# Eight plain products instead of seven recombined ones in the first feed-forward of each layer, with more of the modulation beside it

## The chip, the cores and the metric

The kernel runs on one core of one Trainium2 chip. TensorE (PE) multiplies, VectorE (DVE) and ScalarE (ACT) work on its results and prepare its operands, GpSimd (POOL) does elementwise work and issues some of the transfers, SyncE (SP) issues the others. The metric is the device time of one execution in microseconds (us), median of several runs.

## The reference

One step of a two-layer model on 640 tokens of width 1024: 512 latent tokens and 128 context tokens. Each layer is a feed-forward, a token mixing (a state-space model, attention, a gated MLP) and a second feed-forward. Each is preceded by a norm whose shift, scale and gate come from a conditioning vector through a large linear map, the modulation (`adaln`).

```python
def swiglu_ffn(h, w_in, w_out):
    gate, up = jnp.split(h @ w_in, 2, axis=-1)
    return (jax.nn.silu(gate) * up) @ w_out

def trunk_layer(x, mod, lp, ctx_kv, ssm_init):
    sh1, sc1, g1, sh2, sc2, g2, sh3, sc3, g3 = [mod[:, i][:, None, :] for i in range(N_MOD)]
    h = modulate(rmsnorm(x, lp['norm_ffn1']), sh1, sc1)
    x = x + 0.5 * g1 * swiglu_ffn(h, lp['ffn1_w_in'], lp['ffn1_w_out'])
    ...
    x = x + 0.5 * g3 * swiglu_ffn(h, lp['ffn2_w_in'], lp['ffn2_w_out'])
    return x, ctx_state
```

`w_in` is 1024 x 5632 and `w_out` 2816 x 1024 in each feed-forward, all in float32.

## The kernel before

**Precision.** Every float32 operand is split into a high part, rounded to the engine's fast float32 form, and a low part, the rest. A product is three matmuls (`mm3`, L574): high by high (L578), high by low (L579), low by high (L580). For a weight tile of 128 x 512 ACT makes the high part (L200) and DVE the low part (L208).

**Feed-forward.** The tokens are two halves of 320, A and B. The 2816 hidden columns are 22 units of 128. A block is three to six units: first all their input products ("in"), then the output products of the block ("out"), which are added to `x` by DVE (`accumulate`, L616). The first feed-forward of a layer (f = 0, weights `f0i` and `f0o`) has six blocks of 4, 4, 4, 3, 3 and 4 units, the second (f = 1) four blocks of 6, 6, 6 and 4.

**Seven products.** Most units compute gate and up for both token halves by Winograd's form of Strassen's scheme. The unit is a 2 x 2 problem: two halves of the inner dimension, gate and up columns, token halves A and B. Seven products of 4 `mm3` each (p1 to p7, L869 to L923) replace eight. The price is sums. Sums of the activations are made once (`sums`, L508, called by `all_x_sums`). Sums of the weights are made per unit by transfers that accumulate: POOL issues them onto the loaded tile (`add`, L187, issue at L190), then the tile is split again. Sums of the results are made by ACT copies out of PSUM (L860) and DVE additions (L877 to L921). The first two units of each feed-forward take eight plain products instead: `lead_task` and `lead_rest` in the very first block, `plain_items` in the others.

**Order of the work.** A recorder writes all instructions in one pass. It keeps a model time T, which each `mm3` of 320 columns advances by 0.41 (`clock`, L97). Background work consists of generators that are resumed when T reaches their next due time:

- the modulation (`ada`, L352) is 128 tiles, each one load on SP (L362) and two products with a sum on DVE (L372). A tile comes every `ADA_STEP[stage]` of T: 24 in the input products, 4 in the output products, 12 in the mixing;
- `ssm_build` (L1168) prepares the state-space model of the layer beside its first feed-forward. Much of it is on POOL: 16 passes over the two layers, each with a chain of small operations (L1324 to L1345) that ends in a transfer of the tile `rot`;
- while a "hot" generator is active (a norm, or `all_x_sums`), the others stand still.

Weights are loaded by SP up to nine tiles ahead (`dma`, L169) and split by `splitter` (L219) some 7 of T before they are due. Each engine works through its own list in order, so an instruction that waits holds up all that stand behind it. The 4 PSUM banks `mm` hold the results that are not yet taken away.

Of the kernel before, what the change touches and what calls it, by code (L numbers as in the profile page):

```python
# [32 lines left out]
EARLY = 4  # L33
# [13 lines left out]
           [("sc", 1), ("sh", 1), ("sh", 5), ("sc", 2), ("sh", 2), ("sc", 3)] + [("w", 1)] * 4 +  # L47
           [("sh", 7), ("sc", 4), ("sh", 4), ("sc", 5), ("sc", 6), ("sh", 6), ("sc", 7)] + [("w", 2)] * 6)
SSM_STEP = 5.0
ADA_STEP = {"in": 24.0, "out": 4.0, "mix": 12.0}  # L50
GM1, GM2 = 2.2, 2.2
LEAD, LEAD_HOT = 7.0, 5.0
DMA_LAG, ADD_LAG, HIGH_GAP, HIGH_TO_LOW, LOW_TO_ADD = 5.0, 7.5, 0.7, 0.8, 1.0
# [5 lines left out]
class Kernel:  # L59
# [369 lines left out]
    def norm(self, l, i, X):  # L429
# [5 lines left out]
        p = self.ps("sA")  # L435
# [12 lines left out]
        plain = i != 1  # L448
# [15 lines left out]
        for n in range(KD + 1):  # L464
            yield 1.3
            jobs = []
            if n < KD:
                k = ks[n]
                t = xn.pop(n) if n in xn else dest(k)
                if plain:  # L470
                    hi, lo = self.lead_x(X, k)
# [19 lines left out]
            self.ready[X] = n  # L491
            if plain and n and PLAIN[X][(n - 1) // 4]:
                self.xr[PLAIN[X][(n - 1) // 4]] = (n - 1) % 4 + 1
        if plain and X == "B":
            while not self.whole:
                yield 0.4
            yield from self.all_x_sums()
# [67 lines left out]
    def start_norm(self, nxt, X):  # L565
        self.ready[X] = 0
        self.whole = False
        if nxt[1] != 1:
            self.new_x(*(("11", "21") if X == "A" else ("22", "t1", "t2", "t3", "t4")))
        elif X == "A":  # L570
            self.H = [self.place(n, F32R).rearrange("p (k t) -> p k t", k=2) for n in H_AT]
        self.norms[X] = self.spawn(self.norm(*nxt, X), 2.2, True)
# [53 lines left out]
    def opening(self, ls, stack, ops):  # L626
# [3 lines left out]
        p = self.pool("open", 1, stack=ls)  # L630
# [62 lines left out]

        self.dlimit = 0
        pull()
        self.new_x("11", "21", "22", "t1", "t2", "t3", "t4")
        ps = {}
        for c in range(2):
            for i in range(2):
# [74 lines left out]
        self.have |= {(0, 0), (0, 1)}  # L774
        for n in ("11", "21", "22"):
            self.xr[n] = 4
        for n in ("t1", "t2", "t3", "t4"):
            self.xr[n] = 0

    def lead_x(self, X, k):  # L780

# [6 lines left out]
    def ffn_items(self, l, f, nxt, bg, lead=False):  # L788

        nc = self.nc  # L790
        items = []
# [4 lines left out]
        st = {}  # L796

        def start():
            self.enter("in")
            if not lead:  # L800
                open_hid()
                start_bg()
# [161 lines left out]
        def unit_done(us, X):  # L964
            def done(n, p):
                u = us[n // 2]
                if n % 2 == 0:
                    nc.scalar.activation(temp((u, X)), p, AF.Silu)
                else:
                    v.tensor_tensor(tmp[u, X], tmp[u, X], p, op=ALU.mult)  # L970
                    high(u, X, (u, X), 1.0)
                    low(u, X, (u, X), 1.0)
            return done
# [61 lines left out]
            return [("task", [("fi", l, f, u, f"{r}{h + 1}") for u in us for r in "12"], part(X, h), 8 * len(us) * MM3[HT])  # L1035
                    for X in "AB" for h in range(2)]

        def lead_rest(u):

            def part(n):  # L1040
                def fn(w):
                    p = self.ps()[:, :HT]
                    for k in range(KD):
                        hi, lo = self.lead_x("B", k)
                        self.mm3(p, w[k // 4], slice(k % 4 * 128, k % 4 * 128 + 128), hi, lo, k == 0, k == KD - 1)
                    unit_done([u], "B")(n, p)
                return fn
            return [("task", [("fi", l, f, u, f"{n + 1}{h}") for h in "12"], part(n), KD * MM3[HT]) for n in range(2)]

# [18 lines left out]
        for u in range(NU):  # L1068
            src = {f"{n}{h}": w_in[l, u, j][:, 512 * h:512 * h + 512] for j, n in enumerate("gp") for h in range(2)}
            op = lambda name: ("fi", l, f, u, name)  # L1070

            for n, r, y in (("11", "g0", None), ("12", "g1", None), ("22", "p1", None), ("11e", "g0e", None),
                            ("12e", "g1e", None), ("s1", "p0", "p1"), ("s2", "p0", "g0"), ("s4", "p0", "g1"),
                            ("s3", "g0", "p0")):
                self.ops[op(n)] = (512, op(r), src.get(y))
                self.raws[op(r)] = (src[r[:2]], 512)
            if u < 2:
                self.ops[op("21")] = (512, op("p0"), None)
        for b, (k0, kb) in enumerate(blocks):
            for m in range(KD):  # L1080
# [1 line left out]
        items.append(("call", start))  # L1082
        for b, (u0, kb) in enumerate(blocks):
            us = list(range(u0, u0 + kb))
            if lead and b == 0:
                items.append(lead_task(us[:2]))
                items += lead_rest(us[1])
                items.append(("call", lambda: self.norms.update(B=self.spawn(self.all_x_sums(), 0.0, True))))
                units(us[2:], us[2:])
            else:  # L1090
                items.append(("call", lambda: self.enter("in")))
                if b == 0:
                    items += plain_items(us[:2])
                    us = us[2:]
                units(us, us[:EARLY] if b == 0 else [])
            items.append(("call", lambda: (self.flush(), self.enter("out"))))
            for g in ([0, 1], [2, 3], [4, 5], [6, 7]) if b < n_b - 1 else ([0, 1], [2, 3, 4, 5, 6, 7]):
                if nxt and b == n_b - 1 and g[0] == 2 and nxt[1] == 1:
                    items.append(("call", lambda: self.preload(AF.Gelu_apprx_tanh)))
                for X in "BA" if g[0] == 0 else "AB":  # L1100
                    for m in g:
                        items.append(out_task(m, X, b, kb))
                    if nxt and b == n_b - 1 and m == 7:
                        items.append(("call", lambda X=X: (done(), self.start_norm(nxt, X))))
# [907 lines left out]
```

## Time and profile before

| | |
|---|---|
| median of 3 runs | 2658.41 us (2654.63 to 2659.7) |
| profiled execution, its own time | 2652.66 us |
| its span, from the first to the last instruction | 2650.9 us |
| PE busy | 2415.9 us, 91% |
| DVE busy | 1958.7 us, 74% |
| ACT busy | 1099.2 us, 41% |
| POOL busy | 1049.6 us, 40% |
| granted TensorE clock, mean | 0.964 of full speed |

PE is the busiest engine by far, but its busy share counts matmuls whose pipelined ends are modelled, so 91% does not say that it works at its peak. Where it is slower than elsewhere for the same matmuls has to be read stage by stage. In time the profiled execution lies a little below the fastest of the three runs.

### The profile page before, as it was taken

To read this page: it belongs to the slowest core of one execution; us is meant where nothing else is said; L and a number is where in the kernel's file an instruction comes from. 1 tells how busy PE (TensorE), PEld (TensorE's weight loads), DVE (VectorE), ACT (ScalarE), POOL (GpSimd) and SP (SyncE) were. 2 spreads that over 40 slices of the span, in tenths; PEclk is the share of its full clock that TensorE was granted. 3 is DMA by queue.
4 is the path that set the end of the run, shared out by engine and by line. 5 is a ranking of instruction groups with operands and counts; after the bars stand their busy time and mean duration, and the time that the engine had idled before them with its cause. 6 is when DMAs were issued, how large, how long until landed. Compare 5 with 4: busy or idle time off the path is not lost. (4 is left out here: it accounts for less than half of the span.)

```text
span 2650.9 us, 46542 instructions
## 1 busy us (share of the span) xinstructions
PE 2415.9 (91%) x16492; PEld 2324.6 (88%) x16492; DVE 1958.7 (74%) x4355; ACT 1099.2 (41%) x2517; POOL 1049.6 (40%) x1888
## 2 busy tenths in 40 slices
PE   6779889899999989999998889989998997999999
PEld 5669888799887879999998879888998887999999
DVE  7898688876857778677788977787766578555555
ACT  5424323345444542535354324333544445343533
POOL 5306776752533340211133376867333334121210
PEclk8899999999999999999998999999999999999999
DMA  6557767664443156876745667677353313574753
GB/s 214 133 162 186 174 163 187 160 183 149 141 150 101 57 117 176 191 191 166 193 128 122 153 165 177 174 176 188 101 175 118 113 59 82 134 148 119 155 127 97
DMA packets 193867, 391.36 MB, mean 148 GB/s; under 512 B 31858, under 2 KB 51410, under 8 KB 193636
## 3 DMA queue, kind: packets, MB, share of 16 engines
q1 hardware_dynamic: 132196, 254.94, 29.9%
q0 software_dynamic: 61440, 133.47, 26.0%
q8 instruction: 130, 2.13, 0.3%
q14 instruction: 101, 0.83, 0.1%
HBM read 365.66 MB, written 23.17 MB: 147 GB/s over the span
## 5 line engine op out<-in xcount | busy, mean ns | idle before, releaser
L578 PE MATMUL mm<-hx,w 128*128 128x320 f32 x2928 | 942.5, 322 | 116.7 <-ACT hid L860 30.7
L579 PE MATMUL mm<-hx,w 128*128 128x320 f32 x2928 | 928.1, 317 | 19.3 <-DVE hx L752 10.0
L580 PE MATMUL mm<-hx,w 128*128 128x320 f32 x2928 | 928.3, 317 | 16.6 <-DVE w L208 16.5
L208 DVE TENSOR_TENSOR w<-w 128x512 fp32r<-128x512 f32 (+1 forms) x904 | 625.4, 702 | 237.0 <-ACT w L200 233.1
L200 ACT ACTIVATE w<-w 128x512 fp32r<-128x512 f32 (+1 forms) x904 | 525.4, 608 | 540.5 <-DMA w<-f0i 196.4
L578 PEld LDWEIGHTS mm<-hx,w 128*128 128x128 f32 x2928 | 569.1, 194 | 141.0 <-ACT hid L860 34.9
L579 PEld LDWEIGHTS mm<-hx,w 128*128 128x128 f32 x2928 | 569.5, 195 | 24.3 <-DVE hx L752 11.8
L580 PEld LDWEIGHTS mm<-hx,w 128*128 128x128 f32 x2928 | 568.8, 194 | 23.5 <-DVE w L208 23.5
L578 PE MATMUL mm<-hid,w 128*128 128x320 f32 x1408 | 441.5, 314 | 29.3 <-DVE x L616 24.9
L579 PE MATMUL mm<-hid,w 128*128 128x320 f32 x1408 | 437.7, 311 | 2.3 <-DVE hid L845 2.1
L580 PE MATMUL mm<-hid,w 128*128 128x320 f32 x1408 | 436.8, 310 | 0.0
L190 POOL DMA_DIRECT2D w<-f1i x160 | 142.0, 1019 | 579.3 <-DVE w L208 368.0
L372 DVE SCALAR_TENSOR_TENSOR aj<-ar,sbc 128x1024 bf16<-128x1024 f32 x256 | 315.5, 1233 | 20.6 <-DMA ar<-w_ada 19.7
L616 DVE SCALAR_TENSOR_TENSOR x<-mm,mod,x 128x192 f32<-128x192 f32 (+1 forms) x576 | 231.4, 431 | 110.3 <-PE mm L580 109.8
L578 PEld LDWEIGHTS mm<-hid,w 128*128 128x128 f32 x1408 | 266.6, 189 | 37.8 <-DVE x L616 20.0
L579 PEld LDWEIGHTS mm<-hid,w 128*128 128x128 f32 x1408 | 266.6, 189 | 4.5 <-DVE hid L845 4.5
L580 PEld LDWEIGHTS mm<-hid,w 128*128 128x128 f32 x1408 | 266.4, 189 | 0.0
L190 POOL DMA_DIRECT2D w<-f0i x160 | 147.2, 1016 | 232.1 <-DVE w L208 121.7
L867 ACT ACTIVATE hid<-hid 128x320 f32<-128x320 f32 x148 | 69.8, 471 | 195.9 <-DVE hid L893 135.7
L841 ACT ACTIVATE hid<-hid 128x320 fp32r<-128x320 f32 x176 | 82.6, 470 | 159.3 <-DVE hid L909 69.4
L1792 PE MATMUL mm<-w,hx 128*128 128x256 f32 x480 | 143.8, 299 | 0.0
L1793 PE MATMUL mm<-w,hx 128*128 128x256 f32 x480 | 137.2, 286 | 0.9 <-DVE w L208 0.9
(340 smaller groups left out, 3239.8 us busy)
## 6 DMA issues: line engine op xcount, KB each, us to landing
ar<-w_ada SPq DMA_DIRECT2D x128, 512.0 KB, 4.7
w<-f1i SPq DMA_DIRECT2D x184, 256.0 KB, 3.8
w<-f0i SPq DMA_DIRECT2D x180, 256.0 KB, 3.8
w<-f0i POOLq DMA_DIRECT2D x160, 256.0 KB, 5.5
w<-f1i POOLq DMA_DIRECT2D x160, 256.0 KB, 5.7
w<-f1o SPq DMA_DIRECT2D x96, 192.0 KB, 2.4
w<-f0o SPq DMA_DIRECT2D x64, 256.0 KB, 3.9
w<-wqkv SPq DMA_DIRECT2D x48, 256.0 KB, 4.4
```

The costliest lines, as they stand in the source:

```text
L190: nc.gpsimd.dma_start(raw[r][:, :n], src, accum_op=ALU.add)
L200: nc.scalar.activation(pair[c][0][:, :n], raw[r][:, :n], AF.Copy)
L208: nc.vector.tensor_tensor(lo[:, :n], raw[r][:, :n], hi[:, :n].bitcast(F32), op=ALU.subtract)
L372: nc.vector.scalar_tensor_tensor(jk, r, 1.0, self.sbc[:, c, :], op0=ALU.mult, op1=ALU.mult, accum_out=m[:, c, j * KD + k:j * KD + k + 1])
L578: nc.tensor.matmul(out, hi, rhs_hi, start=start, stop=False, skip_group_check=parts)
L579: nc.tensor.matmul(out, hi, rhs_lo, start=False, stop=False, skip_group_check=parts)
L580: nc.tensor.matmul(out, lo, rhs_hi, start=False, stop=stop, skip_group_check=parts)
L616: nc.vector.scalar_tensor_tensor(self.x[:, m, r0:r1], p[:, r0 - s:r1 - s], self.mod[l][:, c, g * KD + m:g * KD + m + 1], self.x[:, m, r0:r ...
L841: nc.scalar.activation(hid[u, X][0], tmp[src], AF.Copy, scale=sign)
L867: return lambda: nc.scalar.activation(t, t, AF.Silu)
L1792: nc.tensor.matmul(p[:, :256], hh, wh, start=k == 0, stop=False)
L1793: nc.tensor.matmul(p[:, :256], hh, wl, start=False, stop=False)
```

## The change

All units of the first feed-forwards now take eight plain products. `lead_rest` is renamed `plain_unit` and takes a token half; each unit is `plain_unit(u, "A") + plain_unit(u, "B")`, which use the same four split weight tiles. For f = 0 the activation sums, their tiles t1, t2 and t4, the accumulating transfers and the sums of results are gone. t3, which holds a part of B's activations, stays. The second feed-forwards keep their seven products. The modulation gets a new stage name, "plain", for the input products of f = 0, with a tile every 8 of T instead of 24.

```diff
-ADA_STEP = {"in": 24.0, "out": 4.0, "mix": 12.0}
+ADA_STEP = {"plain": 8.0, "in": 24.0, "out": 4.0, "mix": 12.0}
...
-        if plain and X == "B":
+        if i == 2 and X == "B":
             while not self.whole:
                 yield 0.4
             yield from self.all_x_sums()
...
-        def lead_rest(u):
+        def plain_unit(u, X):
 
             def part(n):
                 def fn(w):
                     p = self.ps()[:, :HT]
                     for k in range(KD):
-                        hi, lo = self.lead_x("B", k)
+                        hi, lo = self.lead_x(X, k)
                         self.mm3(p, w[k // 4], slice(k % 4 * 128, k % 4 * 128 + 128), hi, lo, k == 0, k == KD - 1)
-                    unit_done([u], "B")(n, p)
+                    unit_done([u], X)(n, p)
...
-            if lead and b == 0:
-                items.append(lead_task(us[:2]))
-                items += lead_rest(us[1])
-                items.append(("call", lambda: self.norms.update(B=self.spawn(self.all_x_sums(), 0.0, True))))
-                units(us[2:], us[2:])
+            items.append(("call", lambda: self.enter("in" if f else "plain")))
+            if b == 0:
+                if lead:
+                    items.append(lead_task(us[:2]))
+                    items += plain_unit(us[1], "B")
+                else:
+                    items += plain_items(us[:2])
+                us = us[2:]
+            if f == 1:
+                units(us, us[:EARLY] if b == 0 else [])
             else:
-                items.append(("call", lambda: self.enter("in")))
-                if b == 0:
-                    items += plain_items(us[:2])
-                    us = us[2:]
-                units(us, us[:EARLY] if b == 0 else [])
+                for u in us:
+                    items += plain_unit(u, "A") + plain_unit(u, "B")
```

The list of DVE in the input products of layer 1's first feed-forward (block of units 18 to 21): L208 is the low part of a weight tile, L845 the low part of a result, L888, L893, L899, L909 and L918 are the sums and products of the seven-product scheme. Before, about one unit:

```order
L845 SCALAR_TENSOR_TENSOR hid<-hid 128x320
L208 TENSOR_TENSOR w<-w 128x512 x2
L893 TENSOR_TENSOR hid<-mm,hid 128x320
L208 TENSOR_TENSOR w<-w 128x512
L918 TENSOR_TENSOR hid<-hid,mm 128x320
L845 SCALAR_TENSOR_TENSOR hid<-hid 128x320
L208 TENSOR_TENSOR w<-w 128x512
L899 TENSOR_TENSOR hid<-mm,hid 128x320
L208 TENSOR_TENSOR w<-w 128x512
L909 TENSOR_TENSOR hid<-hid 128x320
L208 TENSOR_TENSOR w<-w 128x512
L888 TENSOR_TENSOR hid<-mm,hid 128x320
```

The same place now, from one block of four weight tiles to the next; L968 multiplies silu(gate) by up, L843 is the low part of the result:

```order
L208 TENSOR_TENSOR w<-w 128x512 x4
L968 TENSOR_TENSOR hid<-hid,mm 128x320
L843 SCALAR_TENSOR_TENSOR hid<-hid 128x320
L968 TENSOR_TENSOR hid<-hid,mm 128x320
L843 SCALAR_TENSOR_TENSOR hid<-hid 128x320
L208 TENSOR_TENSOR w<-w 128x512 x4
```

Per unit, seven splits of weights have become four, and five operations on results besides the low parts have become two, one per token half.

The list of POOL in the same feed-forward, one pass of `ssm_build` from the end of one product (L1131) to the small operations (L1330); L190 is an accumulating transfer of the weights, the other DMA rows are the pass's own. Before:

```order
L1131 TENSOR_TENSOR EP<-EP,tp 128x256
L190 DMA w<-f0i 128x512 x2
L1297 DMA dT_16390<-CL 64x2x288 x2
L190 DMA w<-f0i 128x512 x2
L1312 DMA dst_16391<-strip 64x240
L190 DMA w<-f0i 128x512 x2
L1321 DMA dT_16389<-ET 128x512
L1324 MEMSET T 128x2
L1325 MEMSET T 128x2
L1330 COPY T<-ang 128x2 x12
```

Now:

```order
L1131 TENSOR_TENSOR EP<-EP,tp 128x256
L1297 DMA dT_15925<-CL 64x2x288 x2
L1312 DMA dst_15926<-strip 64x240
L1321 DMA dT_15924<-ET 128x512
L1324 MEMSET T 128x2
L1325 MEMSET T 128x2
L1330 COPY T<-ang 128x2 x12
```

No transfer of the weights stands on POOL's list any more in the first feed-forwards; its own chain of work stays.

The list of DVE in layer 0's first feed-forward, in the input products of the block of units 12 to 14, where L372 is the modulation. Now:

```order
L372 SCALAR_TENSOR_TENSOR aj,mod_87<-ar,sbc 128x1024 x2
L968 TENSOR_TENSOR hid<-hid,mm 128x320
L843 SCALAR_TENSOR_TENSOR hid<-hid 128x320
L208 TENSOR_TENSOR w<-w 128x512 x4
L372 SCALAR_TENSOR_TENSOR aj,mod_87<-ar,sbc 128x1024
L968 TENSOR_TENSOR hid<-hid,mm 128x320
L843 SCALAR_TENSOR_TENSOR hid<-hid 128x320
L372 SCALAR_TENSOR_TENSOR aj,mod_87<-ar,sbc 128x1024
```

About a modulation tile and a half (two L372 each) now stand beside a unit. Counted over the whole list, the first feed-forward of layer 0 has 66 of the 128 tiles, the mixing and second feed-forward of layer 0 have 48, and the first feed-forward of layer 1 has 14, all in its first two blocks.

## Rows read from the trace of the kernel before

**Rows 1.** The page's first line.
```profile
span 2650.9 us, 46542 instructions
```

**Rows 2.** Busy time of six-unit input products, layer 1's second feed-forward (us; busy and count; clock; DMA).
```profile
2337.70:2411.70 74.00, 74.00 (x506) 74.00 (x506) 43.63 (x81) 38.43 (x80) 15.78 (x19) 1.00 0.70 156
```

**Rows 3.** The same columns: twelve stretches of input products, first feed-forwards; their sum.
```profile
272.90:342.00 69.10, 55.36 (x350) 53.69 (x349) 47.20 (x91) 26.71 (x55) 51.39 (x116) 0.94 0.73 176
...
1577.50:1644.90 67.40, 55.59 (x350) 54.41 (x349) 45.56 (x89) 26.33 (x55) 50.82 (x105) 0.89 0.74 182
...
1821.10:1876.70 55.60, 53.01 (x350) 51.51 (x350) 38.28 (x73) 26.07 (x55) 31.69 (x74) 0.97 0.73 185
sum 646.90, PE 547.90 PEld 529.30 DVE 485.53 ACT 268.66 POOL 414.89; mean PE 45.66 PEld 44.11 DVE 40.46 ACT 22.39 POOL 34.57
```

**Rows 4.** The same columns: the twelve stretches of output products; their sum.
```profile
140.40:185.90 45.50, 32.00 (x193) 29.98 (x191) 43.12 (x122) 7.18 (x13) 4.32 (x5) 0.92 0.55 156
...
342.00:372.10 30.10, 30.10 (x206) 29.70 (x205) 29.65 (x65) 6.76 (x13) 17.29 (x39) 0.97 0.52 149
416.70:445.10 28.40, 23.90 (x154) 21.53 (x153) 28.05 (x62) 6.05 (x13) 15.53 (x25) 1.00 0.65 162
...
sum 368.30, PE 335.57 PEld 322.82 DVE 342.03 ACT 97.16 POOL 176.40; mean PE 27.96 PEld 26.90 DVE 28.50 ACT 8.10 POOL 14.70
```

**Rows 5.** PE's waits, 1409 to 1906 us (layer 1): us, times, longest.
```profile
PE mm L578 <- ACT hid L860: 15.5, 4, 7.2
PE mm L578 <- ACT w L200: 11.7, 3, 5.1
```

**Rows 6.** POOL in order of time, layer 1, block of units 8 to 11.
```profile
1561.70 0.88 POOL L1321 DMA_DIRECT2D dT<-ET  x1
...
1582.33 0.89 POOL L190 DMA_DIRECT2D w<-f0i  x1 [0.19 <-issue]
...
1586.44 0.58 POOL L1345 DMA_DIRECT2D dT<-rot  x1 [0.30 <-POOL rot L1343]
```

**Rows 7.** ACT in order of time, the same place.
```profile
1586.62 0.63 ACT L200 ACTIVATE w<-w 128x512 fp32r<-128x512 f32 x1 [17.07 <-DMA w<-f0i]
...
1589.63 0.42 ACT L860 ACTIVATE hid<-mm 128x320 f32<-128x320 f32 x1
```

**Rows 8.** PE in order of time, the same place.
```profile
1582.59 0.31 PE L580 MATMUL mm<-hx,w 128*128 128x320 f32 x1
1590.10 0.64 PE L578 MATMUL mm<-hx,w 128*128 128x320 f32 x1 [7.21 <-ACT hid L860]
```

**Rows 9.** PE in order of time, layer 0, input products, just behind two waits.
```profile
307.01 0.47 PE L578 MATMUL mm<-hx,w 128*128 128x320 f32 x1
307.28 0.47 PE L579 MATMUL mm<-hx,w 128*128 128x320 f32 x1
```

**Rows 10.** PE's groups, 1577.5 to 1644.9: `ssm_build`'s matmuls, one pass (count, busy us, mean ns).
```profile
L1304 PE MATMUL sA<-CL,bbd 128*32 128x128 f32 x8 | 0.6, 279 | 0.0
L1317 PE MATMUL sB<-ident,EP 128*128 128x128 f32 x4 | 0.6, 271 | 0.0
```

**Rows 11.** All engines in order of time: the end of a plain unit in the opening.
```profile
83.70 0.49 DVE L970 TENSOR_TENSOR hid<-hid,sA 128x320 f32<-128x320 f32 x1 [0.24 <-PE sA L580]
...
84.22 0.47 ACT L841 ACTIVATE hid<-hid 128x320 fp32r<-128x320 f32 x1 [0.96 <-DVE hid L970]
...
84.73 0.49 DVE L845 SCALAR_TENSOR_TENSOR hid<-hid 128x320 fp32r<-128x320 f32 x1 [0.54 <-ACT hid L841]
```

**Rows 12.** DVE's groups, 272.9 to 342.0 (layer 0, input products): busy us, mean ns.
```profile
L208 DVE TENSOR_TENSOR w<-w 128x512 fp32r<-128x512 f32 x26 | 20.2, 780 | 16.1 <-ACT w L200 16.0
```

**Rows 13.** DVE's groups, 342.0 to 372.1 (layer 0, output products).
```profile
L616 DVE SCALAR_TENSOR_TENSOR x<-mm,mod,x 128x192 f32<-128x192 f32 (+2 forms) x23 | 9.0, 423 | 0.0
L208 DVE TENSOR_TENSOR w<-w 128x512 fp32r<-128x512 f32 x11 | 7.4, 682 | 0.0
```

**Rows 14.** Busy time of L372 alone (four instructions a tile), first feed-forward of layer 0.
```profile
84.00:609.30 525.30, 112.41 (x180) 0.95 0.64 166
```

More of the change, by code (lines that the diff above doesn't have):

```diff
@@ L568, in start_norm @@
         if nxt[1] != 1:
-            self.new_x(*(("11", "21") if X == "A" else ("22", "t1", "t2", "t3", "t4")))
+            self.new_x(*(("11", "21") if X == "A" else ("22", "t3") if nxt[1] == 0 else ("22", "t1", "t2", "t3", "t4")))
         elif X == "A":
@@ L695, in opening @@
         pull()
-        self.new_x("11", "21", "22", "t1", "t2", "t3", "t4")
+        self.new_x("11", "21", "22", "t3")
         ps = {}
@@ L776, in opening @@
             self.xr[n] = 4
-        for n in ("t1", "t2", "t3", "t4"):
-            self.xr[n] = 0
     def lead_x(self, X, k):
@@ L798, in start @@
         def start():
-            self.enter("in")
+            self.enter("in" if f else "plain")
             if not lead:
@@ L1076, in ffn_items @@
                 self.raws[op(r)] = (src[r[:2]], 512)
-            if u < 2:
+            if u < 2 or f == 0:
                 self.ops[op("21")] = (512, op("p0"), None)
```

## The prediction

> **What bounds the kernel now.** I began with the page's head: the span is 2650.9 us [rows 1]; the execution's own time is 2652.66 us, so 1.8 us lie around the span. PE is the engine to watch, and the table of busy time by stage shows where it is slow. In layer 1's second feed-forward a block of 504 matmuls of 320 columns takes 74.0 us, with PE busy in all of it and the clock at full speed [rows 2]. That is 0.147 us a matmul, for seven-product units too, so PE alone sets the time there.
>
> In the first feed-forwards the same matmuls take longer. I cut them into twelve stretches of input products (without the first two, plain units of each layer) and twelve of output products. The input stretches hold 40 units of 7 x 12 = 84 matmuls, 3360 in all, which at 0.147 us need 493.9 us. They take 646.9 us [rows 3]. So 153 us, nearly a quarter, are lost. The output stretches hold 44 units of 48 matmuls, 2112, which need 310.5 us and take 368.3 [rows 4]: 58 us lost.
>
> PE's waits name the cause of the first loss. The largest in layer 1 are for ACT, for copies out of PSUM (L860, 15.5 us) and for high parts of weights (L200, 11.7) [rows 5]. One case in order of time shows what stands behind such a name. POOL's pass of `ssm_build` runs from 1561.70 on; only at 1582.33 does POOL issue the next accumulating transfer of the weights [rows 6]. ACT's next high part needs that sum and starts at 1586.62, after 17.07 us of waiting. The PSUM copy L860, which needs nothing of it, stands behind it and starts at 1589.63 [rows 7]. PE has no bank left and stands for 7.21 us, until 1590.10 [rows 8]. Such a wait costs twice: behind one, matmuls follow each other at 0.27 us [rows 9], which is the lower clock level (1.2 GHz), and the granted clock of these stretches is 0.89 to 0.97 [rows 3] against 1.00 in [rows 2].
>
> **The change, part by part.**
>
> More matmuls: eight products instead of seven are 12 matmuls more for each of 40 units, 480 x 0.147 = **+70.6 us** where PE runs through. The Trainium skill (TensorE: Matmul & The Clock Gate, Back-to-back issue gap) gives N/2.4 + 2.5 ns for a warm matmul, 136 ns at 320 columns, by which the 480 would cost 65 us as an estimate. [Rows 2] show 147 ns for a stream in which each matmul has its own weights, so the measured one is used.
>
> What goes: the accumulating transfers, three splits of weights per unit, the sums of activations and of results. With them goes the chain above: L200 then waits for plain loads, which SP issues up to nine tiles (over two units) ahead, and POOL's pass can run as late as it likes. I take the whole loss of the input stretches as removed, **-153.0**, and put back what has another cause:
>
> - `ssm_build`'s own matmuls: 0.6 + 0.6 us in a pass [rows 10], of which I count 1.0 as not overlapped, 16 passes: +16. They stand on PE in either kernel.
> - The turn from input to output products. The first output task begins with half B, whose last unit has just ended. The opening shows that chain with nothing else in the way: the multiplication starts at 83.70, ACT's high part at 84.22, the low part ends at 84.73 + 0.49 = 85.22 [rows 11], about 1.75 us after PE's last matmul. The output task first has three other units to use, 9 x 0.147 = 1.3 us. That leaves 0.4 us, and at times a modulation product or two in front of it on DVE. A whole modulation tile takes 112.41/45 = 2.5 us [rows 14]. Bounds 0.4 and 2.5; I take 1.0 at each of 12 turns, nearer to the bare chain: +12.
> - In layer 0 DVE leaves each output stretch behind schedule (below), so weights come late at the start of the next input stretch: 5 x 1.5 = +7.5, between 0 and 5 x 3.
>
> Together **+35.5**.
>
> More modulation beside the input products: layer 0's first feed-forward gets 66 tiles instead of 45. DVE pays 2.5 us each. Cover: a four-unit input stretch of layer 0 (384 matmuls, 56.4 us) gives DVE 16 low parts at 0.78 [rows 12] = 12.5 us, eight ends of units at about 0.49 + 0.49 + 0.54 of waiting [rows 11] = 12.2, 52 of T at one tile per 8 = 6.5 modulation tiles = 16.3 and some 10 us of `ssm_build`: 51 of 56.4 us. It fits, with little room; were it gone, each DVE microsecond over would be PE's. So I cost it at nothing here.
>
> Output stretches: nothing in them is changed, but what is late at their start is. DVE has 43.1 busy of 45.5 us in the first, where modulation tiles crowd, and PE gets through only 193 matmuls [rows 4]. With `all_x_sums` gone the modulation starts earlier, nearly all of the eight tiles that this output needs are made beside the input products, and some 5 us of DVE's load and its leftovers from the sums go; I take 34 us, -11.5. In stretches like the one from 416.70 (144 matmuls = 21.2 us, took 28.4 [rows 4]) DVE came late out of the seven-product units; I take -4 for it. In layer 1 the modulation ends in the second block and DVE is light from there: five stretches together about -15 to their matmul time. Sum **-30.5**, between -10 (only the first gains) and -45 (58 less what the norm and `ssm_build` keep).
>
> In layer 0's mixing and second feed-forward the pace of the modulation is as before, 48 tiles, so nothing moves. SP's list loses the repeated loads of early units; its loads of modulation tiles come more densely, but weights are nine tiles ahead.
>
> Sum: 70.6 - 153.0 + 35.5 - 30.5 = -77.4, so 2652.7 - 77.4 = 2575 us by the profiled execution. The median of the runs shown is 5.8 us above that execution, so I predict **2580 us** for the median.
>
> **The rivals.**
>
> 1. *The waits stay (slower).* The trace gives loads and accumulating transfers one name, `w<-f0i`. If ACT's waits were mostly for loads, silu and high parts would stand behind late weights in plain units too. For it: SP serves weights and modulation in one list, and the modulation is denser now. Against it: [rows 6 to 8] fit the accumulating transfer to the microsecond, and the second feed-forward, with as many loads and no POOL chain, has PE busy throughout [rows 2]. If all 153 us stayed and the outputs gained nothing: 2652.7 + 70.6 = 2723. It decides the sign once more than 153.0 - 70.6 + 30.5 = 113 us are lost in place of my 35.5.
> 2. *DVE becomes the bound in layer 0.* My 51 of 56.4 us and 100% in the output stretches (29.65 of 30.10 [rows 4]) leave under 10%. A low part takes 0.780 us beside POOL's work [rows 12] and 0.682 in a stretch with less of it [rows 13]: 14% more. If two-input operations stretch like that in all of layer 0, DVE has about 94 us for 87 us of PE in an input and output pair: 5 x 7 = +35, so 2610 (2615 as a median). The Trainium skill (SBUF — State Buffer, Who interferes with whom) says that a DVE instruction with two inputs in SBUF and a GpSimd instruction that reads SBUF block each other; the longer L208 beside POOL agrees, 0.780 against 0.682 us.
> 3. *POOL's pass becomes the pacemaker.* The model time now runs nearer to PE's, and without waits a pass is due sooner. POOL's chain from 1561.70 to `rot`'s transfer at 1586.44 took 24.7 us [rows 6]; the pauses written in the pass, about 20.5 of T from its start to DVE's next product that reuses that buffer, are 22 us at PE's full pace (0.44 us per 0.41 of T). Without the accumulating transfers in between (the one shown took 0.89) it just about fits. If DVE waits 3 us for it in all 16 passes, +48: 2623, 2629 as a median. PSUM's banks hide part of it, for 10 us of products fit in them.
> 4. *Nothing gained:* losses put back just cancel, 2652.7.
>
> **How the numbers follow.** Forecast 0.67, with a range of its own of 2550 to 2608 (turns 0.4 to 2.5 us, outputs -10 to -45). Rival 2: 0.16, rival 3: 0.08, rival 1: 0.06, rival 4: 0.03. The range 2545 to 2622 leaves out rivals 1 and 4, the worst of 3 and the tails of the first. Differences under 0.2% (5 us) could not be told from none: faster 0.91, same 0.02, slower 0.07.
>
> **What would show it.** In the changed profile, PE's waits for ACT L860 and L200 are gone from the first feed-forwards, their clock is 1.00 outside the first blocks, and a four-unit input stretch takes 58 to 60 us. No L190 on `f0i`. In layer 1 the output stretches take 22 to 30 us, and L372 ends before its third block. I would be wrong if PE waits on silu or weights for more than 5 us at a time (rival 1), if DVE is over 95% busy through layer 0's input stretches with PE waiting on L208 or L616 (2), or if DVE or ACT wait for transfers `dT<-rot` (3).

## The result, and the profile after

The changed kernel takes **2572.93 us** (median of 4 runs, 2565.41 to 2579.98), the kernel before on the same chip 2656.52 us (2654.41 to 2659.7): ratio 0.9684, interval 0.965 to 0.9718. The forecast was 2580, with a range of 2545 to 2622. In a second series the changed kernel took 2572.98 us (4 runs, 2565.52 to 2576.85), ratio 0.9681 [0.9659, 0.9703]. The profiled execution took 2577.15 us. Its page begins so (the span, and the busy time of each engine with its share and its instructions):

```profile
span 2575.4 us, 46281 instructions
...
PE 2446.8 (95%) x16972; PEld 2375.5 (92%) x16972; DVE 1778.2 (69%) x4035; ACT 973.6 (38%) x2253; POOL 850.2 (33%) x1704
```

PE has more to do and the others less; the span is 75.5 us shorter than in [rows 1]. Where these went shows when both spans are cut at the same five places: the opening up to the first matmul behind the plain units, layer 0's first feed-forward, what lies between, layer 1's first feed-forward, the rest. For the kernel after (columns as in [rows 2], count behind each engine):

```profile
0.00:90.75 90.75, 62.40 (x304) 57.76 (x305) 68.60 (x111) 46.09 (x96) 39.48 (x29) 0.85 0.57 200
90.75:561.89 471.14, 457.51 (x3087) 450.59 (x3085) 386.84 (x847) 118.87 (x246) 221.36 (x522) 0.99 0.50 161
561.89:1363.80 801.91, 758.25 (x5359) 730.72 (x5359) 600.28 (x1367) 359.63 (x866) 219.34 (x327) 0.97 0.54 147
1363.80:1826.08 462.28, 453.03 (x3087) 445.94 (x3085) 263.11 (x633) 119.63 (x246) 178.40 (x522) 1.00 0.34 104
1826.08:2575.40 749.32, 715.63 (x5142) 690.50 (x5141) 459.34 (x1081) 329.35 (x799) 191.62 (x306) 0.98 0.47 118
```

The same cut of the kernel before gives 97.21, 512.13, 805.28, 491.67 and 744.61 us. So the opening gained 6.5, layer 0 41.0, the stretch between 3.4, layer 1 29.4, and the rest, where no code changed, lost 4.7. What the opening gained is one wait: in the kernel before PE had finished its plain units at 90.6 us too, and then stood until ACT had the first high part of the seven-product weights. In layer 1 it stood in the same way for 5.08 us, at the end of the stretch between. Before:

```profile
97.21 0.63 PE L578 MATMUL mm<-hx,w 128*128 128x320 f32 x1 [6.58 <-ACT w L200]
```

In each of the two feed-forwards some 240 matmuls more (3087 against 2845 records) are done in less time, at a granted clock of 0.99 and 1.00 instead of 0.95 and 0.95.

Inside the feed-forwards, the stretches of input products after (two of layer 0, two of layer 1) and the sum of all twelve:

```profile
157.66:218.58 60.92, 59.14 (x397) 58.48 (x396) 51.80 (x120) 15.03 (x32) 28.21 (x67) 0.97 0.40 134
248.12:306.65 58.53, 58.53 (x409) 57.74 (x408) 45.59 (x86) 15.99 (x34) 35.86 (x94) 1.00 0.54 171
...
1429.80:1490.42 60.62, 58.76 (x408) 58.00 (x409) 38.14 (x76) 16.22 (x34) 39.07 (x118) 1.00 0.44 138
...
1739.78:1795.93 56.15, 56.15 (x385) 56.15 (x384) 16.10 (x29) 14.62 (x30) 0.00 (x0) 1.00 0.25 76
sum 581.19, PE 576.87 PEld 572.33 DVE 360.30 ACT 152.42 POOL 252.37; mean PE 48.07 PEld 47.69 DVE 30.03 ACT 12.70 POOL 21.03
```

The last row is the floor: 384 matmuls, no wait, 56.15 us, 0.146 us each. The second row, with some 25 matmuls of `ssm_build` more, has PE busy throughout too. Where [rows 3] had 69.10 us at 0.94 there are 58.53 at 1.00, although there is an eighth product. The stretches of output products and their sum:

```profile
118.91:157.66 38.75, 32.64 (x196) 31.45 (x195) 36.57 (x121) 5.82 (x12) 0.00 (x0) 0.91 0.44 143
...
446.91:474.30 27.39, 24.61 (x160) 23.71 (x159) 24.25 (x54) 5.18 (x11) 11.36 (x31) 0.94 0.58 188
...
1391.96:1429.80 37.84, 31.42 (x194) 29.54 (x192) 35.94 (x112) 6.99 (x14) 5.52 (x7) 0.95 0.41 134
...
sum 352.23, PE 333.68 PEld 324.20 DVE 289.65 ACT 86.08 POOL 147.40; mean PE 27.81 PEld 27.02 DVE 24.14 ACT 7.17 POOL 12.28
```

The first one of each layer is still far above its 28.2 us (192 x 0.147), with DVE busy for 36.57 of 38.75 us. PE's waits in layer 1's first feed-forward, which answer to [rows 5], are now (us, times, longest):

```profile
PE mm L578 <- DVE x L616: 4.6, 4, 1.9
PE mm L578 <- ACT hid L839: 4.1, 3, 3.7
PE mm L579 <- DVE hx L489: 2.2, 1, 2.2
```

In neither of the two feed-forwards does PE wait for L860 or L200 any more. The long wait for L839 (ACT's high part of a result) is the turn from input to output products. PE, DVE and ACT in order of time there:

```profile
1393.13 0.31 PE L580 MATMUL mm<-hid,w 128*128 128x320 f32 x1
1397.12 0.59 PE L578 MATMUL mm<-hid,w 128*128 128x320 f32 x1 [3.68 <-ACT hid L839]
```
```profile
1390.96 1.22 DVE L372 SCALAR_TENSOR_TENSOR aj<-ar,sbc 128x1024 bf16<-128x1024 f32 x1
...
1392.92 0.27 DVE L1206 SCALAR_TENSOR_TENSOR ang<-ang 128x112 f32<-128x112 f32 x1
...
1396.09 0.48 DVE L968 TENSOR_TENSOR hid<-hid,mm 128x320 f32<-128x320 f32 x1
```
```profile
1394.58 0.30 ACT L1212 ACTIVATE ang<-ang 128x112 f32<-128x112 f32 x1 [4.67 <-DVE ang L1210]
...
1395.04 0.42 ACT L966 ACTIVATE hid<-mm 128x320 f32<-128x320 f32 x1
...
1396.60 0.47 ACT L839 ACTIVATE hid<-hid 128x320 fp32r<-128x320 f32 x1 [0.63 <-DVE hid L968]
```

PE's last input matmul has started at 1391.81. Half B's multiplication (L968) could start soon after, but it stands on DVE's list behind one modulation product and a chain of small operations on `ang` (`ssm_build`), and begins at 1396.09. The silu that it needs (L966) is late for the same reason: on ACT's list it stands behind an operation of that chain (L1212), which waits 4.67 us for DVE, and begins only at 1395.04. PE does nine matmuls of the other units, then stands for 3.68 us.

### The profile page after: what moved, and what is told of

The parts are those of the page before. It is cut to its first block, busy times and chain, and to the rows that moved or that the text cites. A ratio compares the mean times of both kernels' runs of the same rounds, so it can differ in the third digit from the quotient of the medians.

```text
span 2575.4 us, 46281 instructions
## 1 busy us (share of the span) xinstructions
PE 2446.8 (95%) x16972; PEld 2375.5 (92%) x16972; DVE 1778.2 (69%) x4035; ACT 973.6 (38%) x2253; POOL 850.2 (33%) x1704
## 3 DMA queue, kind: packets, MB, share of 16 engines
q0 software_dynamic: 38400, 91.51, 16.7%
## 5 line engine op out<-in xcount | busy, mean ns | idle before, releaser
L578 PE MATMUL mm<-hx,w 128*128 128x320 f32 x3088 | 977.8, 317 | 30.5 <-ACT hid L935 18.5
L579 PE MATMUL mm<-hx,w 128*128 128x320 f32 x3088 | 968.0, 313 | 18.9 <-DVE hx L752 11.4
L580 PE MATMUL mm<-hx,w 128*128 128x320 f32 x3088 | 967.0, 313 | 10.6 <-DVE w L208 10.6
L208 DVE TENSOR_TENSOR w<-w 128x512 fp32r<-128x512 f32 (+1 forms) x784 | 533.2, 695 | 144.7 <-ACT w L200 141.6
L578 PEld LDWEIGHTS mm<-hx,w 128*128 128x128 f32 x3088 | 590.3, 191 | 45.5 <-ACT hid L935 19.6
L579 PEld LDWEIGHTS mm<-hx,w 128*128 128x128 f32 x3088 | 591.0, 191 | 21.9 <-DVE hx L752 12.9
L580 PEld LDWEIGHTS mm<-hx,w 128*128 128x128 f32 x3088 | 590.9, 191 | 13.2 <-DVE w L208 13.2
L200 ACT ACTIVATE w<-w 128x512 fp32r<-128x512 f32 (+1 forms) x784 | 453.6, 605 | 306.7 <-DVE w L208 132.1
L190 POOL DMA_DIRECT2D w<-f1i x160 | 141.9, 1032 | 582.3 <-DVE w L208 369.2
L616 DVE SCALAR_TENSOR_TENSOR x<-mm,mod,x 128x192 f32<-128x192 f32 (+1 forms) x576 | 232.5, 433 | 142.4 <-PE mm L580 141.4
L372 DVE SCALAR_TENSOR_TENSOR aj<-ar,sbc 128x1024 bf16<-128x1024 f32 x256 | 317.2, 1239 | 19.5 <-DMA ar<-w_ada 18.2
L578 PEld LDWEIGHTS mm<-hid,w 128*128 128x128 f32 x1408 | 266.6, 189 | 21.2 <-ACT hid L839 9.0
L839 ACT ACTIVATE hid<-hid 128x320 fp32r<-128x320 f32 x176 | 83.1, 472 | 378.6 <-DVE hid L968 291.5
L968 DVE TENSOR_TENSOR hid<-hid,mm 128x320 f32<-128x320 f32 x95 | 46.1, 485 | 167.3 <-PE mm L580 164.8
L414 POOL TENSOR_TENSOR acc<-acc,sq 128x320 f32<-128x320 f32 x60 | 62.2, 1037 | 245.7 <-ACT sq L412 237.3
```

Source lines behind the costliest of these rows:

```text
L190: nc.gpsimd.dma_start(raw[r][:, :n], src, accum_op=ALU.add)
L200: nc.scalar.activation(pair[c][0][:, :n], raw[r][:, :n], AF.Copy)
L208: nc.vector.tensor_tensor(lo[:, :n], raw[r][:, :n], hi[:, :n].bitcast(F32), op=ALU.subtract)
L372: nc.vector.scalar_tensor_tensor(jk, r, 1.0, self.sbc[:, c, :], op0=ALU.mult, op1=ALU.mult, accum_out=m[:, c, j * KD + k:j * KD + k + 1])
L414: eng.tensor_tensor(self.acc[X], self.acc[X], q, op=ALU.add)
L578: nc.tensor.matmul(out, hi, rhs_hi, start=start, stop=False, skip_group_check=parts)
```

## The experiments

All were timed against the kernel before on the same chip. Four kernels leave out part of the computation, so their times are those of the work that is left.

**One part of the change alone.** Eight products with the modulation's old pace:

```diff
-ADA_STEP = {"plain": 8.0, "in": 24.0, "out": 4.0, "mix": 12.0}
+ADA_STEP = {"plain": 24.0, "in": 24.0, "out": 4.0, "mix": 12.0}
```

> The changed kernel with the old pace of the modulation beside the plain input products (a tile every 24 of T instead of 8): the eight products alone. If the denser modulation costs and brings nothing, as the prediction costed it, the time stays within 5 us of the changed kernel's 2573 us (2568 to 2578). If it crowds DVE in layer 0 (rival 2 of the prediction), leaving it out gains: 2555 to 2567, with shorter output stretches in layer 0. If it is worth something because layer 1 is freed of the modulation, the time rises to 2580 to 2595, with output stretches of layer 1 longer.

Measured: 2564.68 us (4 runs, 2561.01 to 2567.66), ratio 0.9665 [0.9639, 0.969]. This falls in the range that I gave for rival 2. All the gain is in the products; the denser modulation brings none and seems to cost 5 us by the ratios (8 by the medians), but the intervals overlap (see below for the repetition).

The other part alone, the dense modulation beside seven products:

```diff
-ADA_STEP = {"in": 24.0, "out": 4.0, "mix": 12.0}
+ADA_STEP = {"plain": 8.0, "in": 24.0, "out": 4.0, "mix": 12.0}
...
-            self.enter("in")
+            self.enter("in" if f else "plain")
```

> The kernel before, with seven products, and only the denser modulation beside the input products of the first feed-forwards. DVE there has 47 to 50 us of work in 57 to 69 us; 21 more tiles at 2.5 us are 52 us of DVE work in layer 0. If these fill only gaps, the time stays at 2650 to 2660 us. If seven products leave no room for them, it rises to 2670 to 2700. Under 2640 only if the output stretches of layer 1, freed of 20 tiles, are worth more than I think.

Measured: 2650.32 us (10 runs, 2646.21 to 2657.65), ratio 0.9983 [0.9966, 1.0]: no difference that can be told. Inside, two differences cancel. Layer 0's first feed-forward takes 540.2 us instead of 512.1, so the tiles do not fill gaps only. Layer 1's, with 17 modulation tiles instead of 35, takes 461.2 instead of 491.7, and there PE's waits for L860 fall from 15.5 to 9.0 us and those for L200 from 11.7 to 5.1. So DVE's load feeds the same queue: POOL may add to a tile only when DVE has split it, and in layer 1 POOL's transfers wait 37.2 us for L208 in the kernel before and 26.0 here. Seven products with the modulation spread evenly were not tried.

**What the seven products paid.** The kernel before without the accumulating transfers of the first feed-forwards (their weight sums are not formed, the tiles are split as they are):

```diff
-            nc.gpsimd.dma_start(raw[r][:, :n], src, accum_op=ALU.add)
+            if c[2]:
+                nc.gpsimd.dma_start(raw[r][:, :n], src, accum_op=ALU.add)
```

> The kernel before without the accumulating transfers of the weights in the first feed-forwards: the sums of weight tiles are left out, everything else (seven products, their splits, the sums of results, POOL's pass) stands where it stood. Theory (ACT's high part waits for a transfer that POOL issues late): the input stretches come down from 647 us to about 520 to 545 us, and the time to 2530 to 2560 us. Rival (the waits are for plain loads, or seven products are too tight on ACT and DVE in themselves): the stretches stay above 600 us and the time above 2610.

Measured: 2570.48 us (4 runs, 2566.44 to 2577.52), ratio 0.9695 [0.9661, 0.9729]. The input stretches take 561.1 us, where the same cut of the kernel before gives 634.3. Both lie above what I expected and far below the rival's.

With the transfers, but without POOL's chain of small operations in `ssm_build` (T stays at its initial values):

```diff
-                    for i in range(2):
-                        gp_.tensor_copy(T[:, i, :, 2 ** n], cs[:, 1 - i, n + 1, g])
...
-                    self.cmul(T[:, 0, :, n + 1:n + 1 + q], T[:, 1, :, n + 1:n + 1 + q], T[:, 0, :, 1:1 + q],
-                              T[:, 1, :, 1:1 + q], c[0], c[1], t3[:, :, :q], eng=gp_)
```

> The kernel before without the chain of small operations on POOL in each pass of the state-space model's preparation (copies and complex products that fill one table: that table is left constant); the accumulating transfers stay. Theory (the transfers are late because they stand behind that chain): input stretches 530 to 570 us, time 2545 to 2590 us, near the run without the transfers. Rival (the transfers are slow in themselves, or too many): input stretches above 610 us, time above 2620.

Measured: 2579.01 us (4 runs, 2577.57 to 2580.39), ratio 0.9719 [0.9695, 0.9743]. The input stretches take 559.7 us; both are as expected. The accumulating transfers are all there: in layer 1's first feed-forward, before and here, 164 and 178 GB/s are moved (the last column).

```profile
1414.62:1906.29 491.67, 440.96 (x2845) 426.49 (x2845) 396.57 (x869) 179.76 (x373) 295.33 (x609) 0.95 0.64 164
```
```profile
1378.90:1830.15 451.25, 428.85 (x2845) 417.31 (x2845) 394.13 (x869) 179.79 (x373) 188.07 (x273) 0.98 0.67 178
```

Yet most of their price is gone, because POOL is free to issue them. A lack of DMA bandwidth was thus not the cause, and a DVE held up by POOL's operations hardly: DVE's own busy time in the two first feed-forwards falls by only 6.1 and 2.4 us. PE's waits in layer 1's first feed-forward in that run:

```profile
PE mm L578 <- DVE x L616: 7.2, 7, 2.0
PE mm L578 <- ACT w L200: 5.1, 1, 5.1
PE mm L578 <- DVE hid L899: 3.7, 5, 1.6
```

No wait for L860 is left. The 5.1 us for L200 are the wait at the very start of the layer. It has the same length without the transfers (5.09 us) and without both (5.07), so it does not come from the queue. Both edits at once:

> The kernel before, with neither the accumulating transfers of the first feed-forwards (the weight sums are not formed, their tiles are split as they are) nor POOL's chain (T left at its initial values). Theory: the two cost only together, by queueing behind each other, so without both it is as fast as without the transfers alone, 2563 to 2572 us, and seven products keep a loss of their own (ACT and DVE sums) that eats the 70.6 us that they save on PE. Rival: each has a cost of its own, and without both seven products come near their saving: 2545 us or less.

Measured: 2559.28 us (4 runs, 2555.0 to 2560.96), ratio 0.9645 [0.9622, 0.9668], below what I expected and above the rival's 2545. So against the kernel before (2653.7 and 2654.0 in the two series) the transfers alone give 83 us, the chain alone 75, both 95. If they cost independently, both would give 158; 63 of these are one price, paid when the transfers queue behind the chain, some 20 are the transfers' own and some 12 the chain's. Even so seven products do not come near the 70.6 us that they save on PE. Four of the input stretches of that run, the first two of each layer, tell why:

```profile
92.71:135.30 42.59, 29.79 (x168) 26.68 (x169) 42.04 (x73) 16.21 (x35) 14.34 (x15) 0.84 0.31 106
180.44:237.63 57.19, 53.03 (x349) 51.66 (x349) 49.31 (x132) 26.46 (x57) 13.30 (x23) 0.97 0.44 143
...
1357.13:1390.45 33.32, 29.36 (x169) 27.94 (x170) 30.60 (x53) 15.80 (x34) 10.44 (x11) 0.88 0.41 133
1428.91:1481.94 53.03, 51.49 (x349) 50.34 (x348) 47.04 (x114) 25.22 (x54) 15.76 (x23) 0.99 0.44 141
```

They take 186.1 us for 1008 matmuls, 148.2 at 0.147. In the first, DVE is busy for 42.04 of 42.59 us: here the sums of the activations are made, 23.6 us of it, beside weight splits and modulation. PE waits 8.6 us for these sums (`hx`) there, 2.9 in layer 1. With eight products the first stretch of each layer takes 28.16 us, its floor. Of the 52.4 us that the twelve stretches of this run lose (546.3 against 493.9), 37.9 lie in these four. Seven products freed of the queue take 2559 us, less than the eight of the change with 2573. So the change gains by removing the queue and these starts; that eight products are better in themselves is not shown.

**POOL beside eight products.** The changed kernel without the same chain on POOL:

> The changed kernel without POOL's chain of small operations in the passes of the state-space model's preparation (the table T is left at its initial values). Theory: with eight products nothing waits for POOL, so the time stays: 2568 to 2576 us. Rival 3 of the prediction: if POOL's pass holds up DVE or PE even a little, 10 us or more are gained.

Measured: 2569.69 us (5 runs, 2565.61 to 2574.13), ratio 0.9687 [0.9664, 0.9709], the changed kernel's own in both series. POOL's busy time in the two first feed-forwards fell from 221.4 and 178.4 us to 109.2 and 103.8, and nobody gained by it. What cost 75 us beside seven products is hidden beside eight.

**Turn and pace.** Four kernels on one chip. First the changed kernel itself, whose result is given above:

> The changed kernel itself once more, as the measure for the three runs beside it. About 2573 us (2565 to 2580), 0.969 of before.

Then the old pace again, and half A first at the turn,

```diff
-                for X in "BA" if g[0] == 0 else "AB":
+                for X in "BA" if g[0] == 0 and f == 1 else "AB":
```

and then both:

> Eight products with the modulation's old pace of 24, again. Theory: the denser modulation costs what it adds to DVE in layer 0 (21 tiles x 2.5 us, of which a sixth shows on PE), so about 2565 us and 6 to 10 us below the changed kernel of the same call. Rival: the two intervals so far overlapped by chance and the prediction's cost of nothing was right: within 3 us of the changed kernel.

> The changed kernel, but the first output task of each block in the first feed-forwards begins with token half A. Theory: PE's waits for ACT hid L839 at the turns (0.9, 2.7 and 3.7 us in the profile) come from beginning with B, whose last unit has just ended; with A first they go, and with them the low clock behind: 5 to 12 us less than the changed kernel. Rival: the chain of the last unit is as late for A's third piece or for the results' sums on DVE, the wait moves to another name: within 3 us.

> Both: old pace and half A first. If both effects are real and separate, the fastest of the four, some 12 to 18 us below the changed kernel, about 2557 us. If the turns' waits came from the dense modulation on DVE, no more than 3 us below the run with the old pace alone.

Measured: old pace 2562.19 us (5 runs, 2556.37 to 2568.31), ratio 0.9637 [0.9617, 0.9656]; half A first 2562.93 us (4 runs, 2559.6 to 2566.87), 0.9647 [0.9628, 0.9666]; both 2557.65 us (4 runs, 2556.48 to 2561.01), 0.9629 [0.9611, 0.9646]. The old pace is 10.8 us faster than the dense one, now with intervals that do not meet. In the profiled runs it saves 6.3 us in the two first feed-forwards (465.3 and 460.7 against 469.9 and 462.3). Half A first is 10.1 us faster, as expected, with intervals that overlap a little. It takes 9.9 us off the output stretches (343.4 against 353.3) and leaves the input stretches as they were (579.6 and 578.8). The two gains do not seem to add up (15.3 us together, not 20.9), though the intervals of the last three overlap. PE's waits for L839 in the two feed-forwards say why: 7.6 us in the changed kernel, 2.9 with the old pace, 1.1 with half A first, none with both (a part moves to L616: 7.2 us in layer 1 with half A first, 4.6 before). Both belong partly to the turn, where a modulation product or the `ang` chain delays the last unit.

**The modulation spread evenly.** Half A first with the pace of 8, and a pace of 12 beside the output products (`"outp"`) where it was 4:

```diff
-ADA_STEP = {"plain": 8.0, "in": 24.0, "out": 4.0, "mix": 12.0}
+ADA_STEP = {"plain": 8.0, "outp": 12.0, "in": 24.0, "out": 4.0, "mix": 12.0}
...
-            items.append(("call", lambda: (self.flush(), self.enter("out"))))
+            items.append(("call", lambda: (self.flush(), self.enter("out" if f else "outp"))))
```

> Eight products, half A first at the turns, and the modulation spread evenly over the first feed-forwards: a tile every 8 of T beside the input products and every 12 (not 4) beside the output products. Theory: the first outputs (38.8 us for 28.2 us of matmuls in layer 0) and their neighbours are held by DVE, where the modulation crowds; some 20 tiles x 2.5 us move to input stretches with room, so outputs of layer 0 fall from 171 to about 160 us and the time to about 2550 us. Rival: what holds them is the preparation of the state-space model on DVE and the gate that they need, so 2554 to 2562 us as the run with the old pace and half A first.

Measured: **2539.05 us** (4 runs, 2537.19 to 2542.09), ratio 0.9572 [0.9549, 0.9595], some 30 us below the changed kernel (ratios 0.9572 and 0.9681) and more than I expected. Against half A first alone, from which it differs by the new pace only, it is 20 us by the ratios. Against the old pace with half A first it is 15, and these two have nearly the same amount of modulation beside layer 0's first feed-forward (186 products and 182), so there the place of it is what differs. The outputs of layer 0 take 163.4 us in place of 171.4. The first output stretch of layer 0 with the old pace and half A first, then here:

```profile
118.42:157.21 38.79, 32.67 (x195) 31.45 (x195) 36.63 (x121) 5.82 (x12) 0.00 (x0) 0.91 0.41 144
```
```profile
118.62:150.70 32.08, 29.47 (x196) 28.35 (x195) 29.86 (x109) 5.83 (x12) 0.00 (x0) 1.00 0.36 127
...
sum 329.77, PE 324.12 PEld 318.03 DVE 274.21 ACT 85.99 POOL 153.69; mean PE 27.01 PEld 26.50 DVE 22.85 ACT 7.17 POOL 12.81
```

DVE has 6.8 us less to do (six modulation products instead of twelve, 7.34 us for 14.71) and the stretch is 6.7 us shorter: DVE set its time, and the clock there is now 1.00. The waits of PE that the profile names in the two feed-forwards are down to 2.6 us in layer 0 and 2.8 in layer 1.

The same with a pace of 24 beside the input products:

> As that run, but with a tile only every 24 of T beside the input products: the least modulation of all beside layer 0's first feed-forward, what is left falls to layer 1. By the theory layer 0 is at its best, below 455 us, and layer 1's first feed-forward some 5 us longer: 2550 to 2556 us. If the place of the modulation does not matter beyond layer 0's first outputs, the same as the even one within 3 us.

Measured: 2576.62 us (5 runs, 2576.35 to 2583.18), ratio 0.972 [0.9696, 0.9744], which neither expectation met. Layer 0's first feed-forward takes 451.3 us, as in the even kernel, and layer 1's only 447.5, with PE busy in all of it. But the stretch between takes 830.8 instead of 793.7. What was not made in time is made all at once when it is needed: from 829 to 852 us DVE does seven tiles in a row, ahead of a norm's `rs`, and PE waits for it.

```profile
L372 DVE SCALAR_TENSOR_TENSOR aj<-ar,sbc 128x1024 bf16<-128x1024 f32 x14 | 17.1, 1225 | 3.2 <-DMA ar<-w_ada 2.7
```
```profile
PE sB L426 <- DVE rs L283: 22.7, 1, 22.7
PE mm L578 <- DVE x L616: 12.9, 3, 10.8
```

## Why the prediction held, step by step

**The cause.** It was named rightly: ACT's wait for an accumulating transfer that POOL could not issue. Taking away either side of that queue gives 75 to 83 us. The word "whole" in "the whole loss is removed" covered a second cause, which I did not name: the start of each layer, where DVE makes the sums of the activations, 37.9 us in four stretches. How much of these is the sums alone was not tried. The waits in front of these starts belong to it, too. Of the 11.7 us that [rows 5] give to L200, which I had put down to the transfers, 5.1 are the start of layer 1, and these stay without transfers and without POOL's chain. There ACT's L200 stands behind the high part of the last plain unit (L841). This waits for DVE's multiplication (L970), which stands behind the sums of the activations (L530, L533):

```profile
1411.03 0.48 DVE L530 TENSOR_TENSOR xt<-hx,xn 128x320 f32<-128x320 f32 x1
...
1412.14 0.49 DVE L533 SCALAR_TENSOR_TENSOR xt<-xt,xn 128x320 f32<-128x320 f32 x1
1412.55 0.48 DVE L970 TENSOR_TENSOR hid<-hid,mm 128x320 f32<-128x320 f32 x1
```
```profile
1413.06 0.47 ACT L841 ACTIVATE hid<-hid 128x320 fp32r<-128x320 f32 x1 [2.95 <-DVE hid L970]
1413.44 2.17 ACT L200 ACTIVATE w<-w 128x512 fp32r<-128x512 f32 x4
```

**+70.6.** Right: 0.146 us a matmul in the undisturbed stretch, where the sum has 0.147. By the 136 ns that the Trainium skill gives for a warm matmul by itself (TensorE: Matmul & The Clock Gate, Back-to-back issue gap), those 384 would take 52.2 us as an estimate; they took 56.15.

**-153.0.** Held, but it is two losses. My first stretch began at 90.80, behind the last plain matmul, and the first of its 168 matmuls starts at 97.21: it holds the 6.4 us of that wait, and the first one of layer 1 holds 5.1 more. Cut where the matmuls begin, the first is 43.14 us long and the twelve sum to 634.26, a loss of 140.4. The waits in front are gone after the change too; they are in what the opening and the stretch between gained.

```profile
97.21:140.35 43.14, 31.51 (x168) 28.86 (x169) 42.15 (x73) 16.23 (x35) 18.98 (x20) 0.79 0.51 131
...
sum 634.26, PE 546.59 PEld 527.83 DVE 478.64 ACT 264.17 POOL 413.55; mean PE 45.55 PEld 43.99 DVE 39.89 ACT 22.01 POOL 34.46
```

**+35.5.** Mis-sized. The input stretches after lose 581.2 - 564.5 (3840 x 0.147) = 16.7 us. About 11 of them are `ssm_build`'s matmuls: 145 above 3840, twelve to a pass, so twelve passes, at 0.9 to 1.0 us; the other four passes fall into output stretches. What DVE leaves late at the start of a stretch, for which I had put 7.5, shows almost only in the second stretch of each layer: 60.92 and 60.62 us, where the even kernel takes 57.33 and 58.80. The turns fall behind the cut, into the output stretches: waits for L839 of 0.9, 2.7 and 3.7 us, the low clock behind them, and hardly any for it at the other turns. My 12 for twelve equal turns was about the 9.9 that half A first gave back, but they sit at few turns, where DVE has `ssm_build`'s chain in front. My working had only modulation products in front of it.

**-30.5.** Mis-sized: 369.5 to 352.2 by one cut, -17.3, turns included. The first stretch of layer 0 takes 38.75 us where I took 34. It has fewer modulation tiles than before, but still crowds DVE, as the even kernel shows. Layer 1's five others gave 7.2 us, not the 15 expected: the two short ones came down to 23.3 us and 22.1, near their 21.2, while the three long ones stayed at 30 where their matmuls need 28.2.

**Modulation at nothing.** Wrong by some 5 to 11 us: DVE's sum fits on average (45.59 us busy of 58.53, where I had worked out 51 of 56.4), but not at the turns.

Together the two wrong terms offset each other, and that is luck: inputs and outputs were to be 493.9 + 70.6 + 35.5 + 337.8 = 937.8 us, and are 581.2 + 352.2 = 933.4, with the inputs 18.8 below and the outputs 14.4 above. Some 6 us came on elsewhere, so the profiled execution took 2577 us where the sum gave 2575. The 5.8 us that I added for the median did not come: this profiled execution lies 4.2 us above its median. The inner range of 2550 to 2608 does not follow from the two bounds named beside it either, which give 2558 to 2619.

**The signs.** The waits for L860 and L200 are gone, and L372 ends in layer 1's second block, as said. Of the six four-unit input stretches only one takes 58 to 60 us (58.53). Two take 61, and three take 56.1 to 57.4. In layer 1 the output stretches behind the first take 22 to 30 us; the first takes 37.8.

**The rivals.** Rival 1 (waits stay): none for plain loads. Rival 2 (DVE bound in layer 0): only in the first output stretch and at turns, not throughout; the price was 5 to 11 us, not 35. Rival 3 (POOL as pacemaker): refuted by the run without the chain. The pass that [rows 6] timed, the second of layer 1, takes 12.6 us now from `ET`'s transfer to `rot`'s, instead of 24.7, and the mean of all 16 is 15.6 us instead of 20.2:

```profile
1474.79 0.59 POOL L1321 DMA_DIRECT2D dT<-ET  x1 [4.61 <-ACT w L200]
...
1487.36 0.61 POOL L1345 DMA_DIRECT2D dT<-rot  x1 [0.30 <-POOL rot L1343]
```

## What to carry to other kernels

A scheme that saves matmuls pays in sums on other engines and queues; count its loss in the stretch where it stands, because seven products ran at full speed in the second feed-forwards and lost nearly a quarter of their time in the first, where another engine's chain shared the queue and DVE was full at the start of each layer. Before removing work from the bound engine's neighbours, look whether it is only badly placed: taking the oldest operand first at a turn and spreading the modulation evenly gave another 30 us, the placement about 15 of them. But lazily made work has a due time, and below the rate that meets it the whole remainder lands on the critical path at once.

## What I had not expected of the hardware

The mean of 0.780 us for L208 [rows 12], on which rival 2 rested, is no uniform slowing. Most of the 26 instances took 0.68 or 0.69 us, some 0.76 to 0.9, and one far more. The longest, with POOL's list at the same time:

```profile
301.46 1.94 DVE L208 TENSOR_TENSOR w<-w 128x512 fp32r<-128x512 f32 x1
305.85 0.68 DVE L208 TENSOR_TENSOR w<-w 128x512 fp32r<-128x512 f32 x1
```
```profile
301.14 0.95 POOL L190 DMA_DIRECT2D w<-f0i  x1
301.77 1.07 POOL L1127 TENSOR_TENSOR EP<-EP,tp 128x256 f32<-128x256 f32 x1
```

It lies over a two-input POOL operation of 256 columns and the issue of a transfer. The Trainium skill (SBUF — State Buffer, Who interferes with whom) says that a DVE instruction with two inputs in SBUF contends with a GpSimd instruction that reads SBUF, which fits. Which of the two lengthened this instance is not settled by any run. On the mean, in the same stretch, both edits tell: 0.726 us without the transfers, 0.741 without the chain, 0.692 without both. After the change the chain leaves no trace (0.711 us with it, 0.715 without).

The rest of the program, the same instructions in every eight-product kernel that made its modulation in time, took between 747.5 and 754.8 us, at a granted clock of 0.99 to 0.97: where low-clock pieces fall there differs from kernel to kernel. The runs of the changed kernel spread over 15 us in the same way (2565.41 us at 0.985, 2579.98 at 0.975). Why they fall where they do was not tried, and the 4.7 us that the rest lost in the profile after are within such differences.
